# A hybrid RWKV-7 and convolution decoder layer on one core: the load of the convolution's weights is written ahead of the wait for the shifted copies of its input

## The chip, the cores and the metric

The kernel runs on one core of a Trainium2 chip. The metric is device time in microseconds (us) from the start to the end of one execution. Engines are named as in the profile: PE is TensorE (matmuls), PEld its weight loads, DVE VectorE, ACT ScalarE, POOL GpSimd, and SP SyncE, which in this kernel issues nearly all DMAs, one after the other. An instruction of SP that has to wait holds everything written behind it on SP.

## The reference, cut to what matters

One decoder layer is applied to a prompt of 1024 tokens and to a sample group of 8 sequences of 4 tokens, with D_MODEL 1024. After a normalisation and one input projection the channels split: 512 go through an RWKV-7 recurrence in 8 heads of 64, 512 through a causal depthwise convolution of width 31. One output projection joins them.

```
h = _rms_norm(x, g_pre) * (1 + scale[:, None]) + shift[:, None]
u = h @ w_in
u_r, u_c = u[..., :P_RWKV], u[..., P_RWKV:]
...
y, S_new = _wkv7(s_wkv.astype(jnp.float32), rh, _heads(decay), kh, vh, kk, _heads(a))
...
glu = glu_a * jax.nn.sigmoid(glu_b)
buf = jnp.concatenate([s_conv.astype(dt), glu], axis=1)
conv = lax.conv_general_dilated(
    buf, w_dw[:, None, :], window_strides=(1,), padding='VALID',
    dimension_numbers=('NWC', 'WIO', 'NWC'), feature_group_count=D_CONV) + b_dw
y_c = jax.nn.silu(_group_norm(conv, N_CONV_GROUPS, gn_c_g, gn_c_b, CONV_GN_EPS)) \
    * jax.nn.silu(g_c.astype(jnp.float32))
...
mix = jnp.concatenate([y_r, y_c], axis=-1).astype(dt) @ w_out
```

## The kernel before

Everything is written as strands: Python generators such as `convolutions`, `shifts`, `glu`, `project` and `chain_unit`. A strand puts operations into its own queue and yields. A planner, `_Schedule`, merges the strands while the program is built: it keeps an estimated time for each engine, gives each operation a due time from what it reads and overwrites, and appends the operation that can start first. For a DMA it estimates a landing time. A strand goes on only when all operations that it has queued have been written. So each engine has one fixed order of instructions, and a change in one strand can move instructions of all the others. All instructions come out under one line, L342, so groups are told apart by tile names.

The input projection is the bulk of PE's work: matmuls `ps<-ha` and `ps<-hb` (first and second half of the tokens, the two phases), each product made of three fp32r matmuls with weights split into `whi` and `wlo`. The weights come as `raw<-w_in`, or as kept copies from DRAM (`whi<-kept`, `wlo<-kept`), into 4 buffers for each of `whi` and `wlo`; ACT makes `whi`, POOL makes `wlo`. The output projection (`po<-ha,mh`, `po<-hb,mh` and so on) closes the program.

The convolution of a block of 128 channels (j = 0 to 3) and 256 tokens (g = 0 to 3) goes like this. `glu` writes the gated input to DRAM (`gld`). `shifts` reads it back in four shifted copies of 32 partitions each, four DMAs `SH<-gld`, into one of two halves of the tile `SH`. `convolutions` then runs 32 small matmuls `cv<-SH,wd` (the profile counts 64, two passes for each). `wd` holds the block's weights, 128 x 1024 fp32, 512 KB, loaded by one DMA `wd<-wdd`. There is one buffer for `wd`: a load must wait until the matmuls with the former weights are done. Blocks come in pairs of g by phase, in the phase of the last tokens with a small sample piece (`SH<-gsm`) behind, so there are 8 loads of `wd`, one for each pair (j, phase). The first also waits for the tile's earlier users (`scr`, scratch of the prologue).

Of the other strands these matter here: `chain_unit`, the recurrence, in steps that alternate between PE and ACT, DVE, POOL (`cb<-MV,Q`, then `cb<-Wt,TT`, then `cb<-MV,KTt`, with `Yp` beside them); `inverse_units`, whose `d<-P,TS` needs a DVE result of `p<-TS,AB`; and `post_conv_sample`, which ends in `yc<-cs,arena` of 64 columns.

Of the kernel before, what the change touches and what calls it, by code (L numbers as in the profile page):

```python
# [407 lines left out]
def hymba_step(ctx, tc, xp, xs, cT, ssT, w_ada, badag, gpost, w_in, wup, par, cst, wkv, cvs, w_out, wdd,  # L408
# [85 lines left out]
    def take(tag, name):  # L494

        while all((tag, i) in taken for i in idle[tag]):
            yield BLOCK
        i = next(i for i in idle[tag] if (tag, i) not in taken)
        idle[tag].remove(i)
        t = slot[tag, i]  # L500
        owner[id(t)] = (tag, i, t)
        return t
# [12 lines left out]
    def bank(shape, name, kind="rest"):  # L515

        while not free_banks or not room[kind]:
            yield BLOCK
        i = free_banks.pop(0)
        room[kind] -= 1  # L520
        t = pb.tile(shape, F32, tag=f"b{i}", name=name)
        held[id(t)] = (i, kind, t)
        return t

    def drop(*tiles):
        def fn():
            for t in tiles:
                i, kind, _ = held.pop(id(t))
                free_banks.append(i)
                room[kind] += 1  # L530
        sched.later(fn)

    def mark(key, value=True):
        sched.later(lambda: done.__setitem__(key, value))

    def wait(*keys):
        while not all(k in done for k in keys):
            yield BLOCK
# [1274 lines left out]
    def with_samples():  # L1813

        for j, g, ph in pieces():
            yield j, g, ph
            if g == NU - 1:
                yield j, NU, ph
# [13 lines left out]
    def convolutions():  # L1832


        wd, last = None, None
        for j, g, ph in with_samples():
            yield from wait(("shifts", j, g))
            if (j, ph) != last:
                if last is None:
                    yield from sl.need("wd", 2)  # L1840
                last = j, ph
                wd = w1.tile([128, 1056], F32, tag="wd", name="wd")[:, 0:1024]
                Z.dma_start(out=wd, in_=wdd[j])
                wd = wd.rearrange("p (a t m i) -> p a t m i", a=2, t=4, m=4)
            sh = done["shifts", j, g]
            cv = yield from bank([128, 512], "cv")
            n = UN // 2 if g < NU else 16
            for a in range(2):
                steps = []
                for m in range(4):  # L1850
                    x = sh[:, 4 * a:4 * a + 4, 4 * m:4 * m + UN // 2]
                    if g == NU:
                        x = sh[:, 4 * a:4 * a + 4, 0:NB * 17].rearrange("p c (b x) -> p c b x", x=17)[:, :, :, 4 * m:4 * m + 2]
                    steps += [((cv[32 * c:32 * c + 32, n * a:n * a + n], wd[:, a, c, m, :], x[:, c]),
                               dict(start=(m == 0), stop=(m == 3), tile_position=(0, 32 * c))) for c in range(4)]
                T.batch("matmul", steps)
            sl.free("sh")
            z = (yield from take("nt", "z")) if g < NU else w1.tile([128, 32], F32, tag="as", name="accs")
            for a in range(2):
                o = P_BDW + 2 * j + a  # L1860
                S.activation(z[:, n * a:n * a + n], cv[:, n * a:n * a + n], AF.Identity, scale=0.5, bias=pr[:, o:o + 1])
            drop(cv)
            if g < NU:
                mark(("conv", j, g), z)
            else:
                Z.dma_start(out=accd[:, :, j], in_=z.rearrange("p (a x) -> p a x", a=2))
                mark(("acc", j))
            yield
# [175 lines left out]
    def outputs_sample():  # L2044
# [46 lines left out]
        _Strand("weight_loads", weight_loads()),  # L2091
        _Strand("posts_conv", post_conv(0, 2)),
        _Strand("convolutions", convolutions()),
        _Strand("shifts", shifts()),
        _Strand("glu", glu()),
# [109 lines left out]
```

## Time and profile before

| what | value |
|---|---|
| median of 3 runs | 783.84 us (777.04, 783.84, 787.87) |
| the profiled execution, its own time | 777.9 us |
| its span, first to last instruction | 776.0 us |
| PE busy | 720.3 us, 93% of the span |
| DVE, ACT, POOL busy | 61%, 55%, 50% |
| mean granted TensorE clock | 0.981 |
| DMA on average | 209 GB/s |

The span is what the trace shows in detail; 1.9 us of the profiled execution lie around it. The median of the runs is 5.9 us above the profiled execution. A busy PE is PE with a matmul in flight; its idle time is split by what ended each wait. The granted clock is a share of the full 2.4 GHz; in this trace it is either 1.0 or 0.5, that is 2.4 or 1.2 GHz, and a value between them is a mean over a stretch.

### The profile page before, as it was taken

To read this page: it belongs to the slowest core of one execution; us is meant where nothing else is said; L and a number is where in the kernel's file an instruction comes from. 1 tells how busy PE (TensorE), PEld (TensorE's weight loads), DVE (VectorE), ACT (ScalarE), POOL (GpSimd) and SP (SyncE) were. 2 spreads that over 40 slices of the span, in tenths; PEclk is the share of its full clock that TensorE was granted. 3 is DMA by queue.
4 is the path that set the end of the run, shared out by engine and by line. 5 is a ranking of instruction groups with operands and counts; after the bars stand their busy time and mean duration, and the time that the engine had idled before them with its cause. 6 is when DMAs were issued, how large, how long until landed. Compare 5 with 4: busy or idle time off the path is not lost.

```text
span 776.0 us, 23967 instructions
## 1 busy us (share of the span) xinstructions
PE 720.3 (93%) x9310; PEld 620.4 (80%) x9310; DVE 471.7 (61%) x1125; ACT 427.7 (55%) x1151; POOL 384.4 (50%) x723
## 2 busy tenths in 40 slices
PE   3999997998999989999899999999999999899995
PEld 2668876888889978988888988898898996575774
DVE  3678346863466467665756657769977457626233
ACT  4357765764677455765565556576575454322121
POOL 2455547465548437636521622674773665513222
PEclk9999999999999999999999999999999999899999
DMA  9962799888645773648945794978676586577562
GB/s 309 313 219 80 213 314 308 269 261 248 218 145 163 216 197 99 188 134 225 257 137 164 214 245 120 265 220 231 208 251 233 158 255 183 163 219 258 181 194 82
DMA packets 155185, 162.06 MB, mean 209 GB/s; under 512 B 24096, under 2 KB 117024, under 8 KB 155072
## 3 DMA queue, kind: packets, MB, share of 16 engines
q1 hardware_dynamic: 154784, 160.43, 68.4%
q8 instruction: 73, 1.20, 0.7%
q14 instruction: 40, 0.33, 0.2%
q10 hardware_dynamic: 288, 0.11, 0.1%
HBM read 110.34 MB, written 50.15 MB: 207 GB/s over the span
## 4 chain that ended last, share of the span: by engine, by line
PE 70%; DMA 10%; DVE 8%; ACT 4%; SPq 3%; POOL 3%; issue 2%; DVEq 0%; POOLq 0%; ACTq 0%
PE ps L342 34%; PE po L342 11%; PE cb L342 5%; PE cv L342 4%; SPq L342 3%; PE ap L342 2%; PE Yp L342 2%; PE tp L342 2%; DVE arena L342 2%; PE p L342 1%; ACT arena L342 1%; DMA wa<-w_ada 1%; DVE Q L342 1%; DVE KB L342 1%; PE yc L342 1%
## 5 line engine op out<-in xcount | busy, mean ns | idle before, releaser
L342 PE MATMUL ps<-hb,whi 128*128 128x298 f32 (+3 forms) x928 | 195.3, 299 | 0.0
L342 PE MATMUL ps<-ha,whi 128*128 128x256 f32 (+2 forms) x864 | 180.1, 301 | 3.3 <-ACT ha L342 1.0
L342 PEld LDWEIGHTS ps<-hb,whi 128*128 128x128 f32 x928 | 149.2, 189 | 3.8 <-issue 1.4
L342 PEld LDWEIGHTS ps<-ha,whi 128*128 128x128 f32 x864 | 137.9, 190 | 13.0 <-issue 3.6
L342 PE MATMUL ps<-hb,wlo 128*128 128x258 f32 (+3 forms) x464 | 139.1, 300 | 0.0
L342 POOL TENSOR_TENSOR wlo<-raw,whi 128x512 fp32r<-128x512 f32 x74 | 97.0, 1313 | 75.9 <-ACT whi L342 64.5
L342 PE MATMUL ps<-ha,wlo 128*128 128x256 f32 (+2 forms) x432 | 128.6, 298 | 2.5 <-POOL wlo L342 2.5
L342 PEld LDWEIGHTS ps<-hb,wlo 128*128 128x128 f32 x464 | 87.8, 189 | 2.4 <-issue 1.1
L342 PEld LDWEIGHTS ps<-ha,wlo 128*128 128x128 f32 x432 | 82.3, 190 | 5.4 <-POOL wlo L342 3.2
L342 ACT ACTIVATE X<-AB,cs 32x64 f32<-32x64 f32 x136 | 54.9, 404 | 2.1
L342 ACT ACTIVATE arena<-ps,hp 128x256 f32<-128x256 f32 (+3 forms) x72 | 32.2, 455 | 41.7 <-PE ps L342 29.4
L342 ACT ACTIVATE whi<-raw 128x512 fp32r<-128x512 f32 x74 | 46.0, 626 | 14.2 <-PE ps L342 7.4
L342 ACT ACTIVATE arena<-arena 128x256 f32<-128x256 f32 (+4 forms) x103 | 41.6, 410 | 19.4 <-DVE arena L342 13.0
L342 PE MATMUL cv<-SH,wd 128*32 128x128 f32 (+1 forms) x1280 | 38.0, 272 | 9.5 <-DMA wd<-wdd 3.0
L342 POOL TENSOR_TENSOR arena<-arena,mx 128x256 f32<-128x256 f32 (+2 forms) x32 | 24.5, 766 | 44.7 <-ACT mx L342 39.0
L342 POOL TENSOR_TENSOR tm<-D,Ti 128x15 f32<-128x15 f32 (+4 forms) x135 | 40.5, 300 | 10.1 <-DVE D L342 1.4
L342 POOL TENSOR_TENSOR Ti<-Ti,tm 128x15 f32<-128x15 f32 (+4 forms) x135 | 40.6, 301 | 9.1
L342 DVE SCALAR_TENSOR_TENSOR arena<-ps,pr,arena 128x256 f32<-128x256 f32 (+4 forms) x40 | 17.5, 441 | 41.6 <-ACT arena L342 40.5
L342 PEld LDWEIGHTS cv<-SH,wd 128*32 128x32 f32 x1280 | 33.0, 116 | 11.7 <-issue 8.8
L342 POOL TENSOR_TENSOR ss<-ss 128x1 f32<-128x1 f32 (+1 forms) x17 | 4.3, 252 | 73.1 <-ACT o L342 46.5
L342 PE MATMUL po<-ha,mh 128*128 128x512 f32 x128 | 40.2, 422 | 0.0
L342 DVE TENSOR_TENSOR Q<-arena 64x256 f32<-64x256 f32 (+1 forms) x68 | 37.7, 554 | 0.4
(205 smaller groups left out, 1551.4 us busy)
## 6 DMA issues: line engine op xcount, KB each, us to landing
raw<-w_in SPq DMA_DIRECT2D x66, 256.0 KB, 3.8
kept<-whi SPq DMA_DIRECT2D x36, 256.0 KB, 4.0
kept<-wlo SPq DMA_DIRECT2D x36, 256.0 KB, 3.7
whi<-kept SPq DMA_DIRECT2D x36, 256.0 KB, 3.4
wlo<-kept SPq DMA_DIRECT2D x36, 256.0 KB, 3.7
SH<-gld SPq DMA_DIRECT2D x64, 140.0 KB, 4.3
wa<-w_ada SPq DMA_DIRECT2D x32, 256.0 KB, 5.3
xt<-xp SPq DMA_DIRECT2D x8, 512.0 KB, 6.2
```

The costliest lines, as they stand in the source:

```text
L342: emit = lambda: f(*a, **k)
```

## The change

In `convolutions` the strand waited for the block's shifted copies first and then queued the load of `wd`. Now the load is queued first, as soon as the strand has finished the block before, then the strand yields, and only then does it wait for the copies.

```diff
         for j, g, ph in with_samples():
-            yield from wait(("shifts", j, g))
+
             if (j, ph) != last:
                 if last is None:
                     yield from sl.need("wd", 2)
                 last = j, ph
                 wd = w1.tile([128, 1056], F32, tag="wd", name="wd")[:, 0:1024]
                 Z.dma_start(out=wd, in_=wdd[j])
                 wd = wd.rearrange("p (a t m i) -> p a t m i", a=2, t=4, m=4)
+                yield
+            yield from wait(("shifts", j, g))
             sh = done["shifts", j, g]
```

No instruction is added or taken away on any engine. Up to the first convolution PE's order stays the same; behind it the planner's order differs on all engines. Three places show it.

The first place is on SP, at the load for the fifth pair (block 0, second phase). Before, it stands behind the four copies of its own input, `SH<-gld_78`:

```order
L342 DMA gld_78<-gx 256x1x128
L342 DMA arena<-prj_a_91 128x288
L342 DMA raw<-w_in 128x512
L342 DMA arena<-prj_b_92 128x288
L342 DMA SH<-gld_78 32x8x140 x3
L342 DMA prj_k_88<-arena 128x256
L342 DMA SH<-gld_78 32x8x140
L342 DMA wd<-wdd 128x1024
L342 DMA whi<-kept_163 128x512
```

Now it stands behind the copies of the former block, `SH<-gld_80`, whose convolution still uses the old weights:

```order
L342 DMA raw<-w_in 128x512
L342 DMA SH<-gld_80 32x8x140 x3
L342 DMA raw<-w_in 128x512
L342 DMA SH<-gld_80 32x8x140
L342 DMA arena<-bvd 128x256
L342 DMA prj_r_87<-arena 128x256
L342 DMA wd<-wdd 128x1024
L342 DMA raw<-w_in 128x512
L342 DMA zd<-arena 128x256
```

The load moved ahead by 53 DMAs against the first copy of its own input, and has two DMAs between it and the last copy of the former block. Of the eight loads, those for the pairs 1, 2, 3, 5, 6 and 8 now stand 56, 53, 64, 53, 48 and 15 DMAs ahead of their own first copy; the other two stay where they were, behind or among their own copies.

The second place is on PE, in the fifth group of `inverse_units` (first blocks of the second phase), where `d` needs what DVE makes of `p`. Before, 16 matmuls `ap` stand between them:

```order
L342 MATMUL ps<-hb,whi 128x258 x2
L342 MATMUL p_6035<-TS,AB 32x32 x32
L342 MATMUL ap<-Q,KB 64x128 x16
L342 MATMUL d_6098<-P_6036,TS 32x32 x32
L342 MATMUL ps<-hb,wlo 128x258
```

Now two transposes and 13 matmuls of the projection do:

```order
L342 MATMUL p_5974<-TS,AB 32x32 x32
L342 MATMUL tp<-cs,arena 128x128 x2
L342 MATMUL ps<-hb,whi 128x298 x2
L342 MATMUL ps<-hb,wlo 128x298
L342 MATMUL ps<-hb,whi 128x298 x2
L342 MATMUL ps<-hb,wlo 128x298
L342 MATMUL ps<-hb,whi 128x298 x2
L342 MATMUL ps<-hb,wlo 128x298
L342 MATMUL ps<-ha,whi 128x256 x2
L342 MATMUL ps<-ha,wlo 128x256
L342 MATMUL ps<-ha,whi 128x256
L342 MATMUL d_6080<-P_5975,TS 32x32 x32
```

Between `p` and `d` stood 16 small matmuls, and now stand 15 large ones.

The third place is on PE, in the last unit of the recurrence, first half. Before, its steps are kept apart by output-projection matmuls `po` and by `mp`, a matmul of the sample group:

```order
L342 MATMUL cb<-MV,Q 64x64 x2
L342 MATMUL Yp<-Q,MV 64x64 x2
L342 MATMUL po<-ha,mh 128x512
L342 MATMUL po<-ha,ml 128x512 x2
L342 MATMUL po<-ha,mh 128x512 x3
L342 MATMUL cb<-Wt,TT 64x64 x4
L342 MATMUL mp<-arena,KTt 64x256 x2
L342 MATMUL cb<-MV,KTt 64x64
```

Now they follow each other closely:

```order
L342 MATMUL cb<-MV,Q 64x64 x2
L342 MATMUL Yp<-Q,MV 64x64 x2
L342 MATMUL yc<-cs,arena 128x128
L342 MATMUL cb<-Wt,TT 64x64 x4
L342 MATMUL Yp<-AB,MV 64x64
L342 MATMUL cb<-MV,KTt 64x64 x4
L342 MATMUL Yp<-AB,MV 64x64 x2
L342 MATMUL po<-ha,mh 128x512 x3
```

No `po` or `mp` is left between the steps; what stands there is the unit's own `Yp`, and `yc`.

## Rows read from the trace of the kernel before

**Rows 1.** The page: PE's share, and the chain that ended last, by engine.

```profile
PE 720.3 (93%) x9310; PEld 620.4 (80%) x9310; DVE 471.7 (61%) x1125; ACT 427.7 (55%) x1151; POOL 384.4 (50%) x723
...
PE 70%; DMA 10%; DVE 8%; ACT 4%; SPq 3%; POOL 3%; issue 2%; DVEq 0%; POOLq 0%; ACTq 0%
```

**Rows 2.** Timeline, PE: start, duration, what, count, [idle before <-what ended it].

```profile
124.06 3.13 PE L342 MATMUL cv<-SH,wd 128*32 128x128 f32 x64 [3.05 <-DMA wd<-wdd]
...
186.28 1.95 PE L342 MATMUL cv<-SH,wd 128*32 128x128 f32 x64 [1.08 <-issue]
...
195.47 3.01 PE L342 MATMUL cv<-SH,wd 128*32 128x128 f32 x64 [1.87 <-DMA SH<-gld]
...
275.72 1.95 PE L342 MATMUL cv<-SH,wd 128*32 128x128 f32 x64 [2.10 <-DMA prj_b<-arena]
...
388.91 0.54 PE L342 MATMUL d<-P,TS 32*32 32x32 f32 x40 [2.74 <-issue]
...
455.46 3.43 PE L342 MATMUL cv<-SH,wd 128*32 128x128 f32 x64 [0.39 <-DMA whi<-kept]
...
528.98 1.96 PE L342 MATMUL cv<-SH,wd 128*32 128x128 f32 x64 [0.94 <-DMA gb<-prj_b]
...
674.88 0.44 PE L342 MATMUL yc<-cs,arena 64*128 64x64 f32 x2 [3.73 <-DVE arena L342]
```

**Rows 3.** Timeline, SP: the issue of five loads, and of the first copies.

```profile
116.03 2.04 SPq L342 DMA_DIRECT2D SH<-gld  x4
118.11 0.45 SPq L342 DMA_DIRECT2D wd<-wdd  x1
...
180.00 0.44 SPq L342 DMA_DIRECT2D wd<-wdd  x1
...
269.04 0.45 SPq L342 DMA_DIRECT2D wd<-wdd  x1
...
449.14 0.45 SPq L342 DMA_DIRECT2D wd<-wdd  x1
...
523.03 0.40 SPq L342 DMA_DIRECT2D wd<-wdd  x1
```

**Rows 4.** View of the tile wd, whole span: issues, and time from issue to landing.

```profile
L342 SPq DMA_DIRECT2D wd<-wdd x8: 404/448/1064, 118.1 to 523.0; - x8
...
DMA to landing us min/median/max: 4.5/6.1/6.5
```

**Rows 5.** View of the tile SH, whole span.

```profile
DMA to landing us min/median/max: 3.0/4.4/6.7
```

**Rows 6.** The same view, SP from 116 to 118.1 us: the first four copies.

```profile
DMA to landing us min/median/max: 4.8/5.1/5.3
```

**Rows 7.** Stretches: length, busy (count) PE, PEld, DVE, ACT, POOL; clock; DMA share, GB/s.

```profile
120.00:140.00 20.00, 15.26 (x243) 12.66 (x240) 12.65 (x35) 11.72 (x31) 11.60 (x26) 0.91 1.04 313
...
440.00:460.00 20.00, 18.98 (x323) 17.56 (x322) 10.40 (x26) 12.79 (x37) 5.22 (x13) 0.91 0.93 263
```

**Rows 8.** Timeline, PE: two steps of the recurrence's last unit.

```profile
668.82 0.45 PE L342 MATMUL cb<-Wt,TT 64*64 64x64 f32 x8
...
670.32 0.45 PE L342 MATMUL cb<-MV,KTt 128*64 128x64 f32 x8
```

**Rows 9.** What ended PE's waits (us in total, times, longest): the recurrence.

```profile
PE cb L342 <- DVE MV L342: 0.7, 2, 0.4
```

**Rows 10.** Timeline, PE: two neighbouring pairs of projection matmuls, one `wlo` between.

```profile
118.33 0.40 PE L342 MATMUL ps<-ha,whi 128*128 128x256 f32 x2
...
118.69 0.40 PE L342 MATMUL ps<-ha,whi 128*128 128x256 f32 x2
```

**Rows 11.** The page: making the projection's weights, and their loads' landing.

```profile
L342 POOL TENSOR_TENSOR wlo<-raw,whi 128x512 fp32r<-128x512 f32 x74 | 97.0, 1313 | 75.9 <-ACT whi L342 64.5
...
raw<-w_in SPq DMA_DIRECT2D x66, 256.0 KB, 3.8
```

**Rows 12.** What SP waited for (us in total, times, longest).

```profile
SPq L342 <- PE ps L342: 31.9, 26, 4.4
```

## The prediction

> **What bounds the kernel now.** I read the page first: PE is busy for 720.3 us of a span of 776.0 and makes up 70% of the chain that ended last [rows 1]. So PE's idle time, 55.7 us in all, is what can be won, and the reader is to look in the timeline for the idle time that stands ahead of the convolutions `cv<-SH,wd`. Six of its 20 groups wait noticeably [rows 2]. The one at 195.47 waits 1.87 us for the shifted copies; the load of `wd` had been used there before, so the change has nothing to remove. The other five are each the first group of a pair, the ones that need a fresh `wd`: 3.05, 1.08, 2.10, 0.39 and 0.94 us, together 7.56.
>
> Only the first of the five is put down to `wd`; the others name an unknown or a DMA that the convolution doesn't read. I put them down to `wd` from its landing time. The load takes 6.1 us from issue to landing, 6.5 at most [rows 4]. Added to the issue times [rows 3], this gives 118.11 + 6.1 = 124.2, 180.00 + 6.1 = 186.1, 269.04 + 6.5 = 275.5, 449.14 + 6.1 = 455.2 and 523.03 + 6.1 = 529.1. The groups start at 124.06, 186.28, 275.72, 455.46 and 528.98 [rows 2]. All five fit within 0.3 us, so what ends last in each of these waits is the load that the change moves.
>
> **Part 1: the freed waits.** The load stood right behind its four copies, whose last issue starts about 0.5 us earlier (four take 2.04 us [rows 3]). When the load is long there, the group waits for that last copy alone. For the first group the four copies are known to land after at most 5.3 us [rows 6]: 117.6 + 5.3 = 122.9 instead of 124.06, so 1.1 us is freed, and 1.9 remains. For the other four I take the median of 4.4 us [rows 5]: 183.9, 272.9, 453.0 and 526.9. PE fell idle there at 185.20, 273.62, 455.07 and 528.04 (start less wait [rows 2]), each time later than the copy lands, so these waits go in full. Sum: 1.1 + 1.08 + 2.10 + 0.39 + 0.94 = 5.6 us. What is late next there is nothing on DMA; PE goes on. Bounds: with the longest landing of a copy, 6.7 us [rows 5], the last copies come at 186.2, 275.2, 455.3 and 529.2, and only 1.1 + 0.1 + 0.5 + 0.1 + 0 = 1.8 us is freed. Upwards, the granted clock counts: it is 0.91 in the stretches around the first and the fourth wait [rows 7], and the 64 matmuls of the group took 3.13 and 3.43 us there against 1.95 at the other level [rows 2], so 1.18 + 1.48 = 2.7 us more could come back. I take none of it: the first group still waits 1.9 us, and the group at 195.47 took 3.01 us behind a wait of 1.87 [rows 2].
>
> The Trainium skill, page "DMA: Bandwidth & Descriptors", section "Anatomy of one DMA — SWDGE (gpsimd) path", prices a transfer as about 2.0 us plus its bytes at 436 GB/s, fitted on another issuing path. By that the 512 KB load would land after 3.2 us and a copy of 140 KB after 2.3, and a load issued 0.5 us later would come 1.4 us behind the last copy; the five waits would give back 1.4 + 1.08 + 1.4 + 0.39 + 0.94 = 5.2 us. The measured landings, 6.1 and 4.4 us [rows 4, 5], do not agree with its durations, though the sum hardly differs.
>
> **Part 2: the loads in their new places.** Six of the eight now stand 15 to 64 DMAs ahead of the first copy of their own input, at about half a microsecond an issue 7 to 30 us earlier, more than the 6.5 us of the slowest landing [rows 4]. Two stay where they were, and those two pairs show no wait now. The same bytes move. On SP each load must wait for the convolution that uses the old weights, and holds what is written behind it. For the loads of pairs 6, 7 and 8 this costs nothing, since a DMA that stores the sample piece of that very convolution stands right ahead or nearly so. For pair 1 the tile's former users are long done. I cost Part 2 at 0; it is covered by the weights that lie ready in four buffers, and the price without that cover is the second rival.
>
> **Part 3: the order behind the first convolution.** The planner lays the rest out anew. Most of it I cannot price and take as a draw from the same lot; two differences can be read off the order.
>
> First, `d<-P,TS` at 388.91 waits 2.74 us [rows 2] for DVE's result, 16 small matmuls behind `p`. Now 15 large matmuls stand there. Thirteen of them, at 0.12 us each (three take 118.69 - 118.33 = 0.36 us [rows 10]), are 1.6 us; two transposes and the pipeline bring it near 2. What DVE needs is hidden for that long, against about 1 us before. Bounds: 1 to 2.74 us; I take 2.7, since the `ap` matmuls, whose results also load DVE, are gone from between.
>
> Second, the recurrence. From the start of the last `cb<-Wt,TT` group to `cb<-MV,KTt` lie 668.82 and 670.32 [rows 8]: 0.45 us of matmuls and 1.05 of ACT and DVE work, which other matmuls must cover. I summed up the PE work that the order puts between these two steps, with each kind's mean spacing in the trace: of 32 steps 4 had less than 0.8 us before, now 10 do, between 0.05 and 0.65 us. Against a need of 0.8 us the 10 lack 4.3 us in sum, the 4 lacked 0.8: 3.5 us lost. Bounds: such waits show up for `cb` as 0.7 us in two times [rows 9], 0.35 each, so six more cost at least 2.1; with the full 1.05 us they cost 5.
>
> **The sum** for a profiled execution: -5.6 - 2.7 + 3.5 = -4.8 us on 777.9. The profiled execution lies 5.9 us under the median of the runs, inside their spread of 10.8 us; I put the difference on the median: 783.84 - 4.8 = 779.0 us. That is -0.6%, within the 2% that a measurement of this kernel can tell from no change.
>
> **The rivals.** (a) *The wait only changes its name.* The planner places a convolution by its own idea of when the last input lands. With `wd` out of the sum it will put the group earlier, until it stands ahead of the copies' landing. The group at 195.47, where the weights were there, waited 1.87 us for copies [rows 2]. If all five do so: 5 x 1.87 = 9.35 instead of 7.56 us, +1.8; with -2.7 and +3.5 from Part 3 this is +2.6, 786.4 us. Against it: of the 12 groups that need no fresh `wd`, the timeline shows a wait ahead of that one alone.
>
> (b) *Slower: SP is held.* The place is the load of the fifth pair, two DMAs behind the last copy of the block whose convolution it must wait for. From the end of four copies' issue at 118.07 to the end of the convolution, 124.06 + 3.13 = 127.19, were 9.1 us [rows 2, 3], 8.0 without the wait freed above. Less three issues of 0.5 us, SP would stand still for some 6.5 us, and `raw<-w_in` stands right behind. PE lives on four buffer pairs; one feeds 24 matmuls (two groups of tokens, 12 each) of 0.12 us, 2.9 us, so four last 11.5. A held load comes back after 6.5 us of holding plus 3.8 of landing plus 1.3 of POOL [rows 11], 11.6. It decides as soon as a buffer is empty when the hold starts. The load of the second pair is of the same kind. Twice 6.5 us through to PE, less the 4.8 won: 783.84 + 13 - 4.8 = 792 us. SP does wait for PE now, 31.9 us in 26 waits [rows 12], and PE is hardly ever late for it, which speaks against. The Trainium skill, same page and section, says that a DMA engine does not wait on semaphores and that any wait is served by the issuing sequencer before it dispatches; by that rule this rival exists at all, and the trace agrees, as SP's own waits of 31.9 us show.
>
> (c) *More than that.* Both losses of clock go too (2.7 us), and the wait of 3.73 us ahead of `yc` at 674.88 [rows 2], close before the end, is drawn better: the sample group's `mp` matmuls have moved ahead of that stretch. 779.0 - 2.7 - 3.7 = 772.6 us.
>
> **How the numbers follow.** Forecast 0.48, (a) 0.22, (b) 0.14, (c) 0.16. The likeliest gives 779.0. The range goes down to (c) with the recurrence at its lower bound (2.1 instead of 3.5, 771.2) and 3 us for the place of a median among runs that differ by 10.8, to 768; it goes up to (b), 792. Faster by over 2% (under 768.2) needs (c) and a good draw: 0.06. Slower by over 2% (over 799.5) needs (b) and a bad draw: 0.04. Within 2%: 0.90.
>
> **What would show it.** Part 1 is right if the waits ahead of the groups with fresh weights fall from 7.56 us to about 2, the first to 1.9 with the copies named as what ended it. It is wrong if copies end as long a wait there. Part 3 is right if `d` of the fifth group waits under 1 us and the waits at `cb` grow by some 3 us. (b) would show as SP waiting for `cv` for several us at a load of `wd`, with waits of `ps` for `wlo` behind it. The prediction fails if the new order holds a wait of over 5 us somewhere that has nothing to do with the convolution; of that the order tells nothing.

## The result: slower, by 0.9%

| | before | after |
|---|---|---|
| median of 20 runs each, us | 780.26 (772.88 to 787.87) | 787.40 (778.87 to 793.43) |
| ratio after to before, 95% interval | | 1.0086 (1.006 to 1.0112) |
| profiled execution: time, span, us | 777.9, 776.0 | 788.0, 786.2 |
| PE busy, idle (span less busy), us | 720.3, 55.7 | 730.2, 56.0 |

The medians hold all runs, while the ratios, here and below, leave out runs that lie more than 1.5% above the fastest run of their kernel, so that the two can differ by some tenths of a per cent. The forecast was 779.0 and a gain of 4.8 us. The time is inside the range, but the change lost some 7 us. The first thing to see is on the page of the changed kernel: PE is idle as long as before [rows 1]. Nearly the whole difference of the two spans, 10.2 us, is PE being *busy* for 9.9 us longer with the same 9310 matmuls.

```profile
PE 730.2 (93%) x9310; PEld 626.4 (80%) x9310; DVE 461.7 (59%) x1125; ACT 427.1 (54%) x1151; POOL 388.2 (49%) x723
...
PE 66%; DMA 10%; DVE 8%; ACT 6%; issue 4%; POOL 3%; SPq 2%; DVEq 0%; POOLq 0%; ACTq 0%
```

The waits that the change aimed at are gone. In the view of the convolution's tile `cv`, over the whole span of the changed kernel, PE waits 3.0 us in all, where the six groups of [rows 2] made 9.4:

```profile
its engine sat idle before it (us, times) until:
  DMA SH<-gld: 1.5, 1
  DMA SH<-gsm: 1.5, 1
```

The timeline of PE has the first group where the prediction wanted it, waiting for the copies and for less time, and at the other level of the clock (1.96 us instead of 3.13). It also has waits where there were none, ahead of `ap`, `p` and another `d`:

```profile
123.18 1.96 PE L342 MATMUL cv<-SH,wd 128*32 128x128 f32 x64 [1.53 <-DMA SH<-gld]
...
184.00 1.95 PE L342 MATMUL cv<-SH,wd 128*32 128x128 f32 x64
...
196.52 0.25 PE L342 MATMUL d<-P,TS 32*32 32x32 f32 x1 [1.71 <-issue]
...
388.08 0.75 PE L342 MATMUL d<-P,TS 32*32 32x32 f32 x64
...
461.19 0.44 PE L342 MATMUL ap<-Q,KB 64*64 64x128 f32 x5 [2.92 <-issue]
...
588.59 0.44 PE L342 MATMUL p<-T,AB 32*32 32x32 f32 x15 [1.32 <-issue]
```

("issue" means that the engine waited for nothing that the profile shows.) In the view of what ended PE's waits (us in total, times, longest), the recurrence has grown. The first two rows were 0.2 and 0.7 us in total before, the second of them in [rows 9]; the third was 0.2:

```profile
PE cb L342 <- ACT MV L342: 2.8, 4, 1.2
...
PE cb L342 <- DVE MV L342: 1.7, 4, 0.6
...
PE Yp L342 <- ACT MV L342: 0.8, 2, 0.5
```

SP asks for the weights long before they are used, as the order said. Issues of the first three pairs' weights, against 118.11, 180.00 and 269.04 in [rows 3]:

```profile
77.39 0.38 SPq L342 DMA_DIRECT2D wd<-wdd  x1
...
136.76 0.33 SPq L342 DMA_DIRECT2D wd<-wdd  x1
...
195.58 0.54 SPq L342 DMA_DIRECT2D wd<-wdd  x1
```

### The profile page after: what moved, and what is told of

The parts are those of the page before. It is cut to its first block, busy times and chain, and to the rows that moved or that the text cites. A ratio compares the mean times of both kernels' runs of the same rounds, so it can differ in the third digit from the quotient of the medians.

```text
span 786.2 us, 23971 instructions
## 1 busy us (share of the span) xinstructions
PE 730.2 (93%) x9310; PEld 626.4 (80%) x9310; DVE 461.7 (59%) x1125; ACT 427.1 (54%) x1151; POOL 388.2 (49%) x723
## 4 chain that ended last, share of the span: by engine, by line
PE 66%; DMA 10%; DVE 8%; ACT 6%; issue 4%; POOL 3%; SPq 2%; DVEq 0%; POOLq 0%; ACTq 0%
PE ps L342 32%; PE po L342 12%; PE cb L342 4%; PE cv L342 3%; PE ap L342 2%; PE Yp L342 2%; DVE arena L342 2%; ACT arena L342 2%; PE tp L342 2%; SPq L342 2%; PE p L342 2%; DMA wg<-w_ada 1%; PE ada L342 1%; DVE MV L342 1%; DMA SH<-gld 1%
## 5 line engine op out<-in xcount | busy, mean ns | idle before, releaser
L342 POOL TENSOR_TENSOR wlo<-raw,whi 128x512 fp32r<-128x512 f32 x74 | 98.8, 1337 | 75.0 <-ACT whi L342 63.9
L342 ACT ACTIVATE arena<-arena 128x256 f32<-128x256 f32 (+4 forms) x103 | 41.4, 409 | 17.6 <-DVE arena L342 11.9
L342 POOL TENSOR_TENSOR Ti<-Ti,tm 128x15 f32<-128x15 f32 (+4 forms) x135 | 42.6, 316 | 8.8
L342 ACT ACTIVATE arena<-ps 128x256 f32<-128x256 f32 (+1 forms) x60 | 19.3, 343 | 39.3 <-PE ps L342 39.0
L342 DVE SCALAR_TENSOR_TENSOR arena<-arena 128x256 f32<-128x256 f32 (+1 forms) x50 | 24.1, 489 | 25.6 <-ACT arena L342 23.7
L342 POOL TENSOR_TENSOR st<-st,half 128x4 f32<-128x4 f32 (+3 forms) x35 | 37.1, 1062 | 2.2
L342 PE MATMUL cv<-SH,wd 128*32 128x128 f32 (+1 forms) x1280 | 34.3, 257 | 3.0 <-DMA SH<-gld 1.5
```

The source lines that it names most:

```text
L342: emit = lambda: f(*a, **k)
```

## The experiments

The change does two things at once: it puts eight loads earlier, and it gives the planner another input, whereupon the planner lays out everything behind the first load anew. Theory **order**: the loads gain what the freed waits are worth, and the new order loses more. Rival **loads**: the loads cost, by holding SP or sharing the DMA engines. Rival **no gain**: the wait only passes to the next transfer.

**Two by two.** The first two kernels hold one of the two fixed. A load is written straight into SP's queue at its new (or old) place, and the planner books an instruction that issues nothing where it would have put the load itself. All other rows of all engines are then those of the kernel whose order is kept. Against the kernel before, cut:

```
+    def plan(o):
+        o.emit = lambda: None
+        sched.add(o)
...
-            yield from wait(("shifts", j, g))
-            if (j, ph) != last:
+            turned, told = (j, ph) != last, False
+            if turned:
...
+                told = nth <= 0
+                flat = w1.tile([128, 1056], F32, tag="wd", name="wd")[:, 0:1024]
+                if told:
+                    Z.dma_start(out=flat, in_=wdd[j])
+                    yield
+                else:
+                    nc.sync.dma_start(out=flat, in_=wdd[j])
...
+            yield from wait(("shifts", j, g))
+            if turned and not told:
+                plan(Z._op(nc.sync.dma_start, "dma_start", (), dict(out=flat, in_=wdd[j])))
```

That is *early loads, old order*: `nth` counts the loads, and the planner is told of none. *Late loads, new order* is the changed kernel with the two calls the other way round, `plan(...)` ahead of the wait and `nc.sync.dma_start` behind it.

Expected of early loads in the old order: 

> The eight weight loads stand where the changed kernel has them, but every other instruction of every engine stands in the order of the kernel before. Theory 'order' (the early loads gain what the freed waits were worth, and the new order behind the first convolution loses more): 3 to 9 us under the kernel before, about 774 us beside its 780, with no wait for wd ahead of any group of convolutions. Rival 'loads' (the loads themselves cost, by holding SP or by sharing the DMA engines): 4 to 8 us over the kernel before, 785 to 788, like the changed kernel. Rival 'no gain' (the wait only passes to the next transfer): within 1.5 us of the kernel before.

Expected of late loads in the new order: 

> Every engine's instructions stand in the order of the changed kernel, but the eight weight loads stand behind the shifted copies of their own first piece again. Theory 'order': the changed kernel's 787.4 and the freed waits on top, 790 to 796 us. Rival 'loads': back at the kernel before, 779 to 782. Rival 'no gain': 786 to 789.

Measured: 774.1 us against 778.54 of the kernel before beside it, and 791.27. The second ratio is 1.0175 (1.0119 to 1.0231): the new order is slow with the loads left where they were. Rival *loads* falls with both runs, and *no gain* misses the second by 2 us. The first ratio is 0.9982 (0.9944 to 1.002), so the gain of the loads alone, 4.4 us by the medians and 1.4 by the ratio, is not certain by its interval, and the first run leaves *no gain* standing; two later runs return to it. The view of `cv` in the first kernel shows the freed waits, 3.6 us left of 9.4:

```profile
  DMA SH<-gld: 2.1, 2
  issue: 1.2, 2
  DMA SH<-gsm: 0.3, 1
```

**Other orders, same early loads.** All eight loads stay early in both of the next kernels; the planner is told so for the first one alone, or for all but the first.

```
-                told = nth <= 0
+                told = nth <= 1
```

(`nth != 1` in the other kernel.)

Expected, told of the first: 

> All eight loads stand early; the planner is told so for the first one alone and plans the rest as if they were late, so that the order behind the first convolution is a third one, neither that of before nor that of the change. Theory 'order': a draw of its own, anywhere from 774 to 790 us, with no wait for wd; under 783 or over 790 would show that the order and not the loads carries the loss. Rival 'loads': within 2 us of the changed kernel's 787.4, since the loads stand at the same places. Rival 'no gain': as the kernel before within 2 us.

Expected, told of all but the first: 

> All eight loads stand early; the planner is told so for all but the first, which gives a fourth order. Theory 'order': a draw of its own, anywhere from 774 to 790 us, and not the same as the run that tells it of the first alone (over 3 us apart more likely than not). Rival 'loads': within 2 us of the changed kernel's 787.4. Rival 'no gain': as the kernel before within 2 us.

Measured: 815.94 us, ratio 1.0513 (1.0461 to 1.0565), and 820.4, ratio 1.0557 (1.0504 to 1.0609). That the order carries the loss is shown more crudely than I expected; both lie far outside the 774 to 790 that I allowed for. What they lose is another thing than in the changed kernel, and easy to read. The waits of PE in the first of them begin with

```profile
PE po L342 <- DMA wo<-w_out: 17.6, 7, 3.7
PE po L342 <- DVE o L342: 11.4, 1, 11.4
```

and its stretches from 640 us on (length, busy, clock as in [rows 7]) show a hole:

```profile
640.00:720.00 80.00, 75.25 (x452) 58.38 (x450) 39.11 (x87) 28.02 (x70) 32.78 (x42) 0.96 0.70 199
720.00:780.00 60.00, 29.08 (x141) 18.94 (x142) 9.14 (x15) 6.80 (x16) 5.75 (x9) 0.72 0.35 113
```

The output rows of the samples stream the pieces of `w_out` one by one. In these two orders nothing else lies between the last four pieces, so that piece after piece is waited for, and the granted clock is 0.72 in the mean of that hole (0.69 in the same 60 us of the other kernel). In the kernel before, the 56 us behind 720 have PE busy for 47.4.

**Where the new order loses.** I cut the traces of *early loads, old order* and of the changed kernel where each had done the same amount of matmul work (every matmul counted at the median spacing of its kind in the trace of before). The stretches between the cuts at 428, 536, 632 and 684 us of the first, and their counterparts, take 108.3 and 114.6 us, 96.1 and 97.6, 51.5 and 58.8; up to 428 us both take the same within 0.3, and behind 684 the changed kernel gains 2.9 back. Two stretches hold the loss. Stretches of early loads in the old order:

```profile
427.60:535.90 108.30, 105.85 (x1854) 95.75 (x1854) 77.68 (x208) 67.05 (x197) 58.79 (x127) 1.00 0.79 218
...
632.00:683.50 51.50, 47.63 (x391) 34.06 (x390) 31.34 (x75) 19.65 (x52) 25.02 (x34) 0.93 0.64 177
683.50:773.70 90.20, 79.55 (x374) 58.38 (x372) 33.35 (x51) 17.86 (x46) 23.35 (x37) 0.95 0.55 181
```

The same of the changed kernel:

```profile
427.90:542.50 114.60, 109.64 (x1882) 98.55 (x1881) 76.65 (x216) 65.86 (x195) 58.97 (x131) 0.99 0.75 199
...
640.10:698.90 58.80, 52.94 (x477) 40.23 (x477) 34.86 (x85) 25.52 (x67) 30.39 (x39) 0.88 0.65 191
698.90:786.20 87.30, 77.93 (x373) 58.13 (x371) 28.24 (x39) 16.18 (x43) 20.48 (x32) 0.99 0.55 179
```

The second of the two is the end of the recurrence, where little other work is left. Of its 7.3 us, 2.0 are idle time (5.86 against 3.87, length less busy) and 3.5 are clock (length times what the clock lacks to 1.00: 7.1 against 3.6); the rest is spread over the matmuls. The clock comes back behind it: 0.99 against 0.95 in the last rows, 3.6 us by the same reckoning, more than the 2.9 gained there. Over the whole trace the mean clock is 0.977 in both kernels, so this loss of clock is no part of the net loss. To see whether these places belong to the order, four kernels take the planned sequence from a list, one order up to a cut and the other behind it, all with early loads:

```
+        self.rank[op.key] = self.rank.get(op.key, self.rank.get((s.name, s.count - 2), 0) + 0.5)
...
-                    start = max(self.t[op.eng], op.ready)
-                    if best is None or start < best[0]:
-                        best = (start, rank, op, s)
+                    if best is None or self.rank[op.key] < best[0]:
+                        best = (self.rank[op.key], 0, op, s)
```

Expected, old order to 430 us, then new: 

> All eight loads early in the four runs of this set; only the order of the other instructions differs, written into the kernel as a list. Here the old order up to about 430 us (planned 400) and the new one from there. The profiles of the new order and of the early loads in the old order, laid beside each other at equal matmul work, show the new one level with the old at 428 us, 6.6 us behind at 536, 8 at 632, 15 at 684 and 14 at the end. Theory 'places' (the new order loses at places of its own after 430 us): 786 to 790 us, as the changed kernel. Rival 'start' (what happened before, clock and buffers, sets the loss): 774 to 777, as the old order.

Expected, new to 430, then old: 

> The new order up to about 430 us, the old one from there. Theory 'places': 773 to 777 us, as the early loads in the old order. Rival 'start': 784 to 790, as the changed kernel. The seam itself may add up to 3 us to either.

Expected, old to 530, then new: 

> The old order up to about 530 us (planned 500), the new one from there. Theory 'places': the 6.6 us that the new order loses between 428 and 536 us are spared and the 7.4 behind are not, 781 us (779 to 785 with the seam). Rival 'start': 774 to 777.

Expected, new to 530, then old: 

> The new order up to about 530 us, the old one from there. Theory 'places': the 6.6 us between 428 and 536 us are lost, those behind are spared, 781 us (778 to 784 with the seam). Rival 'start': 785 to 790.

Measured, beside 780.12 us of the kernel before: 784.6, 783.34, 784.07 and 781.76 us, with ratios of 1.0094, 1.0024, 1.004 and 1.0062, each uncertain by 0.33 to 0.46%. One of the ten runs of the first took 1146.65 us, with a mean clock of 0.651; it is the one that was profiled, so its trace is not read. By the times, the third and fourth fit *places* and not *start*, the first comes within 2 us of *places*, and the second misses *places* and comes within 1 us of *start*. So the times decide less than I hoped, and the seams may cost something too. The ratios lean to *places*. With early loads in the old order near 0.997 (0.9982 above, 0.9955 below) and the changed kernel at 1.0086, *places* asks for about 1.009, 0.997, 1.006 and 1.005 (in the third and fourth the old order and the 7.4 or 6.6 us of one place), and only the second lies outside the interval measured, by less than the 3 us that I allowed the seam. *Start* asks for 0.997, 1.009, 0.997 and 1.009; the fourth fits, the third only if the seam cost its 3 us. The traces say more. The end of the recurrence takes 57.0 us with the new order's end behind the old order's beginning (first row below, old to 530 then new), and 51.5 and 51.2 with the old order's end behind the new one's beginning (second and third, cut at 430 and 530):

```profile
639.20:696.20 57.00, 51.89 (x477) 39.43 (x477) 35.06 (x84) 24.73 (x65) 31.29 (x39) 0.91 0.65 193
```
```profile
637.30:688.80 51.50, 47.63 (x392) 34.03 (x391) 31.51 (x75) 19.89 (x51) 24.82 (x34) 0.93 0.61 177
```
```profile
645.20:696.40 51.20, 46.92 (x392) 33.48 (x391) 31.43 (x75) 19.77 (x51) 24.76 (x34) 0.97 0.63 175
```

This place belongs to the order's end, whatever ran before. The other, 428 to 536 us, is less clear: behind the new beginning the old order takes 110.5 us there, between 108.3 and 114.6, and in the kernel before, the old order with late loads, it takes 112.2 (431.7 to 543.9 us). A warning goes with such cuts: up to about 430 us the second mixture has the new order, as the changed kernel has, yet its trace comes to the first cut at 432.3 us and that of the changed kernel at 427.9. Two profiles of one order can be 4 us apart.

**A nudge to the planner, and the loads once more.** The planner's constant for the lag between engines, 0.3, was set to 0.301 and to 0.299 with the loads left late; then 0.301 with early loads, by the means of the first experiment; and early loads in the old order were run again.

```
-    LAG = 0.3
+    LAG = 0.301
```

Expected, lag 0.301: 

> The kernel before, loads late, with the planner's lag constant at 0.301 in place of 0.300: nothing is changed but the order, which leaves that of before at about 115 us and shares most of it. Theory 'order' (the planner's order alone moves the time by as much as the change did, without any change of the loads): somewhere in 772 to 792 us, 3 us or more away from the kernel before. Rival 'robust' (orders of equal planned end are worth the same): within 2 us of the kernel before.

Expected, lag 0.299: 

> The kernel before, loads late, with the lag at 0.299. The planned order ends as in the two runs in which the planner was told of a part of the early loads (the samples' output rows last, alone). Theory 'order': 810 to 825 us with no change of the loads at all, 30 to 45 over the kernel before, with the waits for the pieces of the output weights one after another at 720 to 755 us. Rival 'loads' for those two runs: within 10 us of the kernel before.

Expected, early loads in the old order again: 

> The early loads in the old order once more, the same kernel, for the size of the direct gain, which the first set left between -4.4 us (medians) and none (its interval). Theory: 4 to 6 us under the kernel before of the same set. Rival 'no gain': within 1.5 us.

Expected, early loads with lag 0.301: 

> The order of the kernel before with lag 0.301, and the eight loads early in it: a second pair of kernels that differ in the loads alone. Theory: 3 to 6 us under the run with lag 0.301 and late loads. Rival 'no gain': the same within 1.5 us; rival 'loads cost': 3 us or more over it.

Measured, beside 779.82: 779.86, 806.26, 776.8 and 778.57 us. Lag 0.301 is no different from before, 0.9969 (0.9923 to 1.0016), so here *robust* was right and *order* missed. Lag 0.299 costs 3.2%, ratio 1.0318 (1.0234 to 1.0401), with no change of the loads; 4 us less than my lower end. The mechanism that I named is there, but it makes up 9.1 of the 33.7 us between its span, 809.7, and that of the kernel before:

```profile
PE po L342 <- DMA wo<-w_out: 9.1, 7, 1.9
```

The rest was not taken apart. Behind 720 us the granted clock is 0.86 in that trace (to 809) and 0.97 in the kernel before (to 776).

For the loads by themselves there are now four pairs that share their order, each kernel taken against the kernel before of its own set: 774.1 - 778.54 = -4.4 us, 776.8 - 779.82 = -3.0, 778.57 - 779.86 = -1.3, and in the new order (787.40 - 780.26) - (791.27 - 778.54) = -5.6. The mean is -3.6. The ratios are weaker: 0.9982, 0.9955 (0.9907 to 1.0003) and 0.9976 (0.9932 to 1.002) for the early kernels, the last no lower than its late partner's 0.9969; only in the new order, 1.0086 against 1.0175, do the intervals lie apart, and those two kernels were measured in different sets. In us the ratios come to -1.4, -3.5, +0.5 and -6.9, in the mean -2.8. My 4 to 6 us for the second run in the old order were not reached, and of the pair with lag 0.301 *no gain* was right. So early loads cost nothing and gain a few us at most; that they gain time in the old order is likely, but not shown. Early loads in the old order have the lowest medians of this study, at the edge of what can be measured.

## Why the prediction was wrong

**Part 1, the freed waits, held as far as the waits go.** Of 7.56 us ahead of the groups with fresh weights, 1.53 remain, in the first group, with the copies named; I had said about 2 and 1.9. With the order fixed, the waits at `cv` fell from 9.4 to 3.6 us, and of the 7.56 again only the first group's wait is left:

```profile
126.45 3.09 PE L342 MATMUL cv<-SH,wd 128*32 128x128 f32 x64 [1.78 <-DMA SH<-gld]
```

The time gained is smaller than the 5.6 us that I put down: 3.6 in the mean of four pairs by the medians, 2.8 by the ratios. The means lie above my lower bound of 1.8, but single pairs lie below it (1.3 by the medians, 1.4 and none by the ratios). Of the clock I took nothing. The stretch of 120 to 140 us did come back from 0.91 to 1.00 in the changed kernel, but stayed at 0.91 in both traces with the order fixed, where the first group took 3.09 and 1.95 us.

**Part 2, the loads in their new places, held.** SP waits for `cv` 3.0 us in five times in the whole changed kernel, 1.3 at most, where rival (b) needed twice 6.5; and the runs with early loads in two old orders are not slower than before:

```profile
SPq L342 <- PE cv L342: 3.0, 5, 1.3
```

Rival (a) fell too: the groups were not pulled ahead of their copies, since only 3.0 us of waiting is left. The rule of the Trainium skill by which I weighed the load (page "DMA: Bandwidth & Descriptors", section "Anatomy of one DMA — SWDGE (gpsimd) path": about 2.0 us plus the bytes at 436 GB/s, fitted on another issuing path, an estimate of 3.2 us here) is again not met; the two loads of the changed kernel whose landing the trace tells took 4.4 and 4.7 us. It changed nothing in the sum.

**Part 3, the order, is the step that failed**, and in it the clause "Most of it I cannot price and take as a draw from the same lot". The two differences that I did read off came near. The `d` of the fifth group waits no more (388.08). The waits at `cb` grew from 0.9 to 4.5 us, 3.6 more, where I had 3.5. What I had set to zero is the rest of the order, and it cost more than all that I priced. By the two-by-two experiment the new order costs 12.7 us with late loads (791.27 - 778.54; 13.6 by the ratio), and 10.1 to 11.5 with early ones (787.40 - 780.26 = 7.1, plus the 3.0 and 4.4 that early loads gain in the old order; 8.1 and 10.2 by the ratios). Less 3.6 - 2.7 = 0.9 us for what I had priced in it, some 7 to 13 us stood at zero. Between the traces of the two orders with early loads, 773.7 and 786.2 us, 4.7 us are idle time, with new waits that I hadn't looked for (2.92 at `ap`, 1.71 at another `d`, 1.32 at `p`), and 7.8 are PE busy for longer with the same matmuls. My own mark of failure, one new wait of over 5 us, missed it: the largest of the three is 2.92, and PE's idle time in all is what it was before the change.

Zero looks wrong as a mean, too. Of the five other orders that were run whole, one, which shares most of its places with the old one, is as fast (lag 0.301), that of the change is 1.75% slower with late loads, and three are 3.2 to 5.6% slower (two of them with early loads). None is faster. But five are few, and those three share one fault, the pieces of `w_out` waited for one by one, so they are hardly three draws.

That the time still lies inside the range is luck. The -4.8 us were put on a median of three runs, 783.84, and 20 runs gave 780.26; on that base the forecast would have been 775.5, and 787.40 lies 11.9 us above it. It is luck, too, that rival (a) named 786.4, since the waits that it named did not come.

**What stays open.** From the early loads in the old order to the changed kernel PE is busy 7.8 us longer (722.4 and 730.2). The list of instruction groups tells where most of it lies: in two groups of the recurrence, `ap` and `Yp<-AB,MV` (count, busy us, mean ns of one). Early loads in the old order:

```profile
L342 PE MATMUL ap<-Q,KB 64*64 64x128 f32 x544 | 23.6, 281 | 0.9 <-DVE KB L342 0.8
L342 PE MATMUL Yp<-AB,MV 64*64 64x64 f32 x256 | 18.6, 237 | 0.3 <-ACT MV L342 0.3
```

The changed kernel:

```profile
L342 PE MATMUL ap<-Q,KB 64*64 64x128 f32 x544 | 27.0, 286 | 2.9 <-issue 2.9
L342 PE MATMUL Yp<-AB,MV 64*64 64x64 f32 x256 | 21.8, 241 | 1.3 <-ACT MV L342 0.8 <-DVE MV L342 0.2
```

A single matmul takes hardly longer, but fewer of them overlap. A group's busy time may overlap with another group's; counting only what each matmul adds to PE's busy time, the two groups still make up 4.9 of the 7.8 us. In the trace the 544 `ap` stand in 28 unbroken runs in the old order and in 49 in the new one, the 256 `Yp` in 58 and 76. With late loads it is the same, so it belongs to the order: 23.5 and 18.6 us in the kernel before, 26.2 and 21.6 in the new order. As to why, a candidate is that the new order passes from one kind of matmul to another more often: 1060 times against 978, counted in the traces by output tile and shape. That would be 0.1 us a change. This is only argued: no run changes the number of passages alone. Four of the five groups with fresh weights in [rows 2] named something other than `wd`. For three of them the trace has the landing of their own load, 6.1, 6.5 and 6.2 us behind its issue at 180.00, 269.04 and 449.14 [rows 3], that is at 186.1, 275.5 and 455.3, 0.1 to 0.2 us ahead of the group. For the group at 528.98 it has none; that it too waited for `wd` rests on its wait vanishing with the order fixed.

## What to carry to other kernels

Where a planner sets the order, moving one transfer is two changes. Freeze the order and move the transfer alone, then change the order alone; only the first has a price that can be read from a profile. The order at hand may be a good draw, as it was here: without a row that prices the re-layout, lean towards a loss, and allow for a few per cent (the five other orders here cost between nothing and 5.6). And look at PE's busy time as well as its waits: most of this loss was longer busy time, which no list of waits shows, while the list of instruction groups does.

## What the hardware showed unexpectedly

The load of `wd`, 512 KB, mostly lands sooner where it does not stand right behind shifted copies on the queue. The traces tell the landing of some of the loads only. In the kernel before, three loads right behind their copies took 6.1, 6.5 and 6.2 us from issue to landing; the fourth that is known, issued at 494.62 us with another DMA between it and the last copy, took 4.5, the lowest of [rows 4]. Behind copies, one load in the new order with late loads took 5.9 and one with lag 0.301 took 7.1. The two known loads of the changed kernel stood apart from copies:

```profile
DMA to landing us min/median/max: 4.4/4.6/4.7
```

With early loads, five in the old order took 3.4 to 4.9 us, and six with lag 0.301 took 3.5 to 5.8. So a late load was not only asked for late but mostly also some 1 to 2 us slower, while the copies themselves hardly changed (median 4.4 us before [rows 5], 4.6 in the changed kernel). No run changes a load's neighbours alone: the place and the other transfers of the moment change with them.
